# A hybrid block on one core: one more up pair in seven-product steps, three gated products on VectorE, one table load later

## The chip, the cores and the metric

The kernel runs on one NeuronCore of a Trainium2 chip. The metric is device time in microseconds (us); lower is better. Five engines work side by side, each through its own queue in order: TensorE (PE in the profile, its weight loads PEld), VectorE (DVE), ScalarE (ACT), GpSimd (POOL) and SyncE (SP, which here only issues DMAs). Operands lie in SBUF, products of TensorE land in PSUM banks.

## The reference

One layer on 512 tokens of width 1024: a short gated convolution and a forgetting attention are merged through gates, and a channel mixer follows. The change touches the mixer (FFN_HIDDEN is 2816, so 22 blocks of 128 in each half):

```python
    x = x + (g_conv * y_conv + g_attn * y_attn) @ w_o[l]
    h = rms_norm(x, norm_ffn_g[l])
    up = causal_dwconv(h @ w_up[l], conv_ffn_w[l])
    a, b = jnp.split(up, 2, axis=-1)
    x = x + (jax.nn.silu(a) * b) @ w_down[l]
    return rms_norm(x, norm_f_g)
```

## The kernel before

Tokens lie along the free axis (512), features along the partitions in blocks of 128. **Each product is made of three.** A float32 operand is split in a high part (ScalarE copies it to a rounded type, line 275: `wh_...`) and a low part (VectorE subtracts, line 279: `wl_...`); TensorE adds high x high, low x high and high x low. Weights come in chunks (`stream`, in order): a DMA of SP fills a `raw` buffer, `split` makes `wh` and `wl`, and TensorE uses them. There are two `wh` and two `wl` buffers, so the `wh` of a chunk can only be written when TensorE has finished with the `wh` of the chunk two before it.

**Plain pairs.** Pair j of the mixer is block j of `a` and block j of `b`. A plain pair is two chunks of 1024 columns, `up{2j}` and `up{2j+1}` (`block`), each 48 matmuls of 128x128 by 256 columns into one bank. VectorE then scales the bank (line 1170, `fz`), ScalarE and VectorE make the three taps of the convolution (lines 566, 567, 570, `fu`), and `glu` gates: Silu on ScalarE (line 1231), the product of an even pair on GpSimd (line 1236, `ge`), that of an odd pair too (line 1243, `go`), but for the last pair of a phase, whose product is put off and made by VectorE.

**Seven-product pairs** (those in `SUP`). Two output blocks by two input blocks by two halves of the tokens are made with seven products where a plain form takes eight. A step has a chunk P (768 columns, 18 matmuls) and a chunk F (1024 columns, 24 matmuls); a pair takes two steps, 84 matmuls in all, into the four banks 2 to 5. Their weights are sums of weight blocks. F chunks are made in DRAM by chains of DMAs, some of which add (`make_forms`: SP issues the copies at line 208, GpSimd the adds at line 211; `slot` sets when, two slots for each pair, one for each `wo` chunk in front of them and one for each down step). Their inputs are the "x forms", combinations of the rows of x1 that lie in slots 0 to 15 of `gh` and `gl` in phase 1 (`up_forms`). After the second step `merge` puts the banks together (ScalarE line 1191; VectorE lines 1192 to 1213), and the taps and `glu` follow as for a plain pair.

**Phases.** Phase 0 is pairs 0 to 11, then 12 down steps. Phase 1 is pairs 12 to 21, then the nine down steps of `STEPS[1]`, all in the seven-product form. A down step (i, q) takes as moving operands the forms of group q, that is of pairs 2q and 2q+1: seven combinations of `ge{q}` and `go{q}`, which VectorE makes (lines 1253, 1254, 1257, 1258, called t1, t3, t2, t4 below) and which are split in turn in `gh` (line 1262) and `gl` (line 1263). The first down step of phase 1 uses q = 6 and 7, the second uses q = 8 and 9, so pairs 16 to 19. Down steps are numbered through the whole program: before, those of phase 1 are P34/F34 to P42/F42.

**What sets the order.** Matmuls and conversions stand as written. Evacuations, taps and forms wait in a list `later`: each has a chunk number from which it is due and a cost in us, and `split` empties some of it behind each chunk, up to a budget (1.7 us for an `up` chunk, 1.6 for P, 0.75 for F; with evacuations waiting 4.2, 1.6 and 1.2). What a step needs is emptied at the latest by `flush` in front of it. A table load of ScalarE's Sqrt for the last norm is forced by the activation at line 1233, behind the Silu of pair 21.

Of the kernel before, what the change touches and what calls it, by code (L numbers as in the profile page):

```python
# [8 lines left out]
F32 = mybir.dt.float32  # L9
F32R = mybir.dt.float32r  # L10
AF = mybir.ActivationFunctionType
# [7 lines left out]
H = 8  # L19
# [3 lines left out]
NP = FFN // P  # L23
# [34 lines left out]
PLAIN = [(m, k) for m in (6, 7) for k in range(*PHASES[1])]  # L58
PCUTS = (0, 8, 12, 20)

SUP = ((1, 2, 5), (14, 16))
XF = (26, 0)
UPD = tuple(tuple(((j, q), (j, q + 1)) for j in js for q in (0, 2)) for js in SUP)
DOUBLES = GATES + UPD[0] + STEPS[0] + UPD[1] + STEPS[1]
# [6 lines left out]
def block_kernel(ctx, tc, xT, vecs, wv, win, wmix, wo, wup, wst, wdp, outT):  # L71
# [3 lines left out]
    nc = tc.nc  # L75
# [6 lines left out]
    def keep(ins):  # L82
        return tc.keep_in_program_order(ins)

    def bank(i, name):
        return ps.tile([P, S], F32, tag=f"b{i}", name=name)

    def ring(*ids):
        st = [0]

        def f(name):
            st[0] += 1
            return bank(ids[(st[0] - 1) % len(ids)], name)

        return f
# [13 lines left out]
    tbl = cp.tile([4 * H, 1], F32, tag="tbl", name="tbl")  # L109
# [19 lines left out]
    def step_chunks(n):  # L129
        m = len(DOUBLES[n])  # L130
        return [(f"P{n}", wst[n, :, : 3 * m * P], 3 * m * P), (f"F{n}", n, 4 * m * P)]
# [10 lines left out]
    for ph, (j0, j1) in enumerate(PHASES):  # L142
        for j in range(j0, j1):
            if j in SUP[ph]:
                stream += step_chunks(n) + step_chunks(n + 1)
# [10 lines left out]
    later = []  # L156
# [33 lines left out]
    def make_forms(n0, n1, key, start=0):  # L190

        size, step, shift = GROUPS[key]
        if not start:
            make_forms.slot = 0
        cuts = [n0]
        for n in range(n0 + 1, n1 + 1):
            if n == n1 or n - cuts[-1] == size or len(DOUBLES[n]) != len(DOUBLES[cuts[-1]]):
                cuts.append(n)
        for g, (a, b) in enumerate(zip(cuts, cuts[1:])):
            m = len(DOUBLES[a]) * P  # L200
            f = dr.tile([P, b - a, 4 * m], F32, tag=f"f{a}", name=f"f{a}")
            w = wst[a:b].rearrange("n p c -> p n c")
            x0, x1, x2 = w[:, :, 3 * m : 5 * m], w[:, :, 5 * m : 7 * m], w[:, :, 7 * m : 8 * m]
            for n in range(a, b):
                made[n] = f[:, n - a, :]

            def put(dst, src):
                return lambda: keep(nc.sync.dma_start(dst, src))

            def add(dst, src):  # L210
                return lambda: keep(nc.gpsimd.dma_start(dst, src, accum_op=ALU.add))  # L211

            f0, f1, f2 = f[:, :, : 2 * m], f[:, :, 2 * m : 3 * m], f[:, :, 3 * m :]
            ops = (put(f0, x0), add(f0, x1), put(f1, f[:, :, :m]), add(f1, x1[:, :, m:]), put(f2, f1), add(f2, x2))
            todo_bg.extend((start + (step * k if isinstance(step, int) else step[k]) + shift * g, op) for k, op in enumerate(ops))
        todo_bg.sort(key=lambda w: w[0])

    def slot():

        while todo_bg and todo_bg[0][0] <= make_forms.slot:  # L220
            todo_bg.pop(0)[1]()
        make_forms.slot += 1
# [14 lines left out]
    def flush(banks=None):  # L237

        def wanted(w):
            return set(w[2]) & set(banks) if banks is not None else True  # L240

        while any(map(wanted, later)):
            n = next(n for n, w in enumerate(later) if banks is None or wanted(w) or w[0] < len(parts))
            with after_split():
                later.pop(n)[3]()

    def flush_only(tags):

        while n := [n for n, w in enumerate(later) if set(w[2]) & set(tags)]:
            with after_split():  # L250
                later.pop(n[0])[3]()
# [84 lines left out]
    eps = ex[:, NT : NT + 1]  # L336
# [347 lines left out]
    for t in range(NT):  # L684
        src = pa[t][:, 4 * HD : VW].unsqueeze(1).to_broadcast([P, 4, H])
# [61 lines left out]
    acc, bank_s, bank_t = ring(2, 0, 1), ring(3, 4), ring(5, 6)  # L747
# [25 lines left out]
    k = len(parts) + 2  # L773
# [90 lines left out]
    acc = ring(3, 4, 5, 6, 2, 7)  # L864
# [41 lines left out]
    k = [c[0] for c in stream].index("mix0")  # L906
# [52 lines left out]
    for j in range(KB):  # L959
# [13 lines left out]
        else:  # L973
            if j == GJ:
                acc = ring(3, 4, 2, 7)
# [10 lines left out]
        a, b = gs  # L986
# [13 lines left out]
    gh = gx.tile([P, NG, 2 * P], F32R, tag="gh", name="gh")  # L1000
# [6 lines left out]
    acc = ring(0, 1, 5, 6, 3, 4, 2, 7)  # L1007
# [116 lines left out]
    def turns(*ids):  # L1124
        st = list(ids)

        def f(name):
            f.last = st.pop(0)
            flush((f.last,))
            return bank(f.last, name)  # L1130

        return f

    acc = turns(0, 1, *(2, 3, 4, 5) * 2, 6, 7, 0, 1, 2, 3, 4, 5)
    USETS = dict.fromkeys(SUP[1], (2, 3, 4, 5)) | {1: (2, 3, 4, 5), 2: (6, 7, 0, 1), 5: (6, 7, 0, 1)}
    ssq3 = xp.tile([P, S], F32, tag="ssq", name="ssq3")

    def place(ph, q):
        return (16, 24, 32, 0, 8)[q - PHASES[1][0] // 2] if ph else q * NF

    def up(j, ph, rb2, pu=None):
# [6 lines left out]

        if j in SUP[ph]:
            c = 2 * SUP[ph].index(j)  # L1150
            slot()
# [74 lines left out]
    def glu(ph, j, uu):  # L1226
        a, b = uu
        q, k = j // 2, len(parts) - 1
        g0 = place(ph, q)
        with tc.issue_after(order["hi"]) if j + 1 == PHASES[ph][1] else ExitStack():  # L1230
            nc.scalar.activation(a, a, AF.Silu)
        if j == NP - 1:
            nc.scalar.activation(tbl, a[: 4 * H, :1], AF.Sqrt, scale=0.0, bias=eps[: 4 * H])
        if j % 2 == 0:
            ge = glu.even = fp.tile([P, 2, 2 * P], F32, tag="ge", name=f"ge{q}", bufs=2)
            keep(nc.gpsimd.tensor_mul(ge, a.rearrange(halves_of, h=2), b.rearrange(halves_of, h=2)))  # L1236
            return
        flush_only([("q", x) for x in range(q)])
        ge = glu.even
        go = fp.tile([P, 6, 2 * P], F32, tag="gr", name=f"go{q}")  # L1240

        def mul(eng):
            return eng.tensor_mul(go[:, 0:2, :], a.rearrange(halves_of, h=2), b.rearrange(halves_of, h=2))

        if j + 1 < PHASES[ph][1]:
            keep(mul(nc.gpsimd))
        else:
            later.append((k + 3, 0.7, (("q", q),), lambda: mul(nc.vector)))
        b11, b12 = ge[:, 0, :], ge[:, 1, :]
        b21, b22, t1, t2, t3, t4 = (go[:, i, :] for i in range(6))  # L1250

        def t13():
            nc.vector.tensor_sub(t1, b11, b12)
            nc.vector.tensor_sub(t3, b22, b12)

        def t24():
            nc.vector.scalar_tensor_tensor(t2, t1, -1.0, b22, op0=ALU.mult, op1=ALU.subtract)
            nc.vector.scalar_tensor_tensor(t4, t2, -1.0, b21, op0=ALU.mult, op1=ALU.subtract)

        def hl(src, gs):  # L1260
            def f():
                nc.scalar.activation(gh[:, gs, :], src, AF.Copy)
                nc.vector.tensor_sub(gl[:, gs, :], src, gh.bitcast(F32)[:, gs, :])

            return f


        d = (2, 3, 4) if j + 1 < PHASES[ph][1] else (4, 5, 6)
        w = [(d[0], 0.85, t13), (d[0], 0.85, t24), (d[1], 0.7, hl(ge[:, : 1 + ph, :], slice(g0, g0 + 1 + NF * ph, NF)))]
        w += [(d[x > 0 and 2 or 1], 0.7, hl(go[:, x : x + 2, :], slice(g0 + 1 + x, g0 + 3 + x))) for x in (0, 4, 2)]  # L1270
        at = next((x for x, i in enumerate(later) if ("e",) in i[2]), len(later))
        later[at:at] = [(k + n, us, (("q", q),), f) for n, us, f in w]

    def combine(ph, i, banks, ids):

# [46 lines left out]
    X, Y = (6, 7, 0, 1), (2, 3, 4, 5)  # L1322
    for ph, (j0, j1) in enumerate(PHASES):
        if ph:
            acc = turns(*(6, 7, 0, 1) * 4)
            make_forms(ND[1], len(DOUBLES), ph)
        for j in range(j0, j1):
            pu = None
            if j == 0:
                nrm = {}  # L1330

                def mid():
                    nrm["c"] = rstd_col([ssq2], NT, 6, "n2")

                def late():
                    nrm["b"] = rstd_sb(rstd_bc(nrm["c"], NT, 7, "n2"), "n2")

                pu = lead(["up0", "up1"], x1h, x1l, mid, late)
            up(j, ph, nrm["b"], pu)
        if not ph:  # L1340
            up_forms(0, 1)
        flush_only((("e",),))
        seven(
            STEPS[ph], ND[ph], ({0: X, 1: Y, 3: X, 2: Y}, {0: X, 1: Y, 2: Y})[ph],
            lambda q, g: (gh[:, place(ph, q) + g, :], gl[:, place(ph, q) + g, :]),
            done=lambda i, banks, ids: combine(ph, i, banks, ids), tick=True,
        )
        assert not todo_bg
# [188 lines left out]
```

## Time and profile before

| | |
|---|---|
| three runs | 692.52, 692.88, 693.15 us; median 692.88 |
| the profiled execution | 693.81 us, its span 692.0 us |
| granted clock, mean | 0.998 |
| VectorE, ScalarE, GpSimd busy | 80%, 53%, 28% of the span |
| plain pairs of phase 1 | 12, 13, 15, 17, 18, 19, 20, 21 |
| seven-product pairs of phase 1 | 14, 16 |

How to read the views: in a timeline a row has its start, its length (both us), engine, line, operation, tile written <- tiles read, shapes and, in brackets, how long the engine was idle before it and who released it. Lengths of neighbouring VectorE rows overlap by about 0.08 us, so the cost of one in a full queue is the distance to the start of the next. A row of the stages has the stretch, its length, then busy us and instructions of each engine, the granted TensorE clock, the DMA share and GB/s. A row of the waits has engine, tile and line that waited, who released it, total us, times, longest. A row of the chain has start, length, engine, tile and line.

### The profile page before, as it was taken

The numbers are of one execution on the slowest core, as the hardware profiler recorded it, in microseconds if no ns is written. First come the engines' busy times: TensorE is split into PE (matmuls) and PEld (weight loads), VectorE is DVE, ScalarE is ACT, GpSimd is POOL, SyncE is SP. The second block draws the span as 40 slices with busy tenths as digits, with TensorE's granted clock in tenths as the row PEclk, the third lists the DMA queues.
The fourth block names the chain that finished last, engine by engine and source line by source line (L and its number), as shares of the span: only waits on it lengthen the run. The fifth ranks groups of instructions, "written<-read, shape, count | busy, mean of one in ns | idle before, by whom it ended". The sixth has DMA issues, their size and how long they took to land.

```text
span 692.0 us, 14716 instructions
## 1 busy us (share of the span) xinstructions
PE 683.5 (99%) x5936; PEld 681.6 (98%) x5936; DVE 554.6 (80%) x860; ACT 368.4 (53%) x581; POOL 192.8 (28%) x204
## 2 busy tenths in 40 slices
PE   9999999999999999999999999999999999999996
PEld 9999999999999999999999999999999999999996
DVE  6677887967578778868879699998786899988894
ACT  5575755555555444446554455546444544546572
POOL 6124946542020201214400144340100324332000
PEclk9999999999999999999999999999999999999999
DMA  8628999563577586798997498888944997775613
GB/s 310 219 68 286 220 241 206 127 136 92 168 160 214 162 265 196 234 310 215 165 312 237 123 252 211 190 229 254 262 141 150 314 243 169 197 168 147 205 31 123
DMA packets 66165, 137.54 MB, mean 199 GB/s; under 512 B 5888, under 2 KB 31760, under 8 KB 65840
## 3 DMA queue, kind: packets, MB, share of 16 engines
q1 hardware_dynamic: 45384, 107.28, 46.7%
q0 software_dynamic: 18896, 26.03, 23.8%
q10 hardware_dynamic: 1816, 3.29, 1.3%
q8 instruction: 46, 0.75, 0.4%
q14 instruction: 23, 0.19, 0.1%
HBM read 132.31 MB, written 47.71 MB: 260 GB/s over the span
## 4 chain that ended last, share of the span: by engine, by line
PE 88%; DVE 7%; DMA 2%; ACT 1%; issue 1%; POOL 0%; DVEq 0%; ACTq 0%; POOLq 0%
PE dn L327 26%; PE p_up L309 15%; PE p_in L309 14%; PE p_wo L309 6%; PE p_up L327 4%; PE yc L309 3%; PE ya L309 3%; PE pa L477 2%; DMA y<-ys 2%; PE pb L479 2%; PE p_q L309 2%; PE p_k L309 2%; PE o L658 2%; DVE wl_up L279 1%; PE tp L641 1%; DVE fu L567 1%
## 5 line engine op out<-in xcount | busy, mean ns | idle before, releaser
L211 POOL DMA_DIRECT2D f<-in_wst_dram x69 | 80.3, 1349 | 25.6 <-DMA f<-f 25.3
L309 PE MATMUL p_up<-x1h,wh_up 128*128 128x256 f32 x416 | 81.1, 276 | 0.0
L309 PE MATMUL p_up<-x1l,wh_up 128*128 128x256 f32 x416 | 81.1, 276 | 0.0
L309 PE MATMUL p_up<-x1h,wl_up 128*128 128x256 f32 x416 | 81.0, 276 | 0.0
L279 DVE TENSOR_TENSOR wl_F<-raw_F,wh_F 128x1024 fp32r<-128x1024 f32 (+1 forms) x43 | 56.0, 1303 | 21.6 <-ACT wh_F L275 21.6
L275 ACT ACTIVATE wh_F<-raw_F 128x1024 fp32r<-128x1024 f32 (+1 forms) x43 | 44.4, 1034 | 41.5 <-PE dn L327 27.2
L309 PEld LDWEIGHTS p_up<-x1l,wh_up 128*128 128x128 f32 x416 | 62.7, 188 | 0.0
L309 PEld LDWEIGHTS p_up<-x1h,wh_up 128*128 128x128 f32 x416 | 62.7, 188 | 0.0
L309 PEld LDWEIGHTS p_up<-x1h,wl_up 128*128 128x128 f32 x416 | 62.6, 188 | 0.0
L309 PE MATMUL p_in<-xgh,wh_in 128*128 128x256 f32 x288 | 56.8, 279 | 0.0
L309 PE MATMUL p_in<-xgh,wl_in 128*128 128x256 f32 x288 | 56.6, 278 | 0.0
L309 PE MATMUL p_in<-xgl,wh_in 128*128 128x256 f32 x288 | 56.5, 278 | 0.0
L279 DVE TENSOR_TENSOR wl_P<-raw_P,wh_P 128x768 fp32r<-128x768 f32 (+1 forms) x43 | 41.9, 974 | 13.7 <-ACT wh_P L275 7.9
L275 ACT ACTIVATE wh_P<-raw_P 128x768 fp32r<-128x768 f32 (+1 forms) x43 | 35.3, 821 | 31.2 <-PE dn L327 23.3
L1236 POOL TENSOR_TENSOR ge<-fu,fu 128x512 f32<-128x512 f32 x11 | 20.1, 1829 | 111.8 <-DVE fu L570 86.7
L327 PE MATMUL dn<-gh,wh_F 128*128 128x256 f32 x216 | 51.0, 276 | 0.0
L327 PE MATMUL dn<-gl,wh_F 128*128 128x256 f32 x216 | 51.0, 276 | 0.0
L279 DVE TENSOR_TENSOR wl_up<-raw_up,wh_up 128x1024 fp32r<-128x1024 f32 x34 | 43.8, 1288 | 7.5 <-ACT wh_up L275 7.5
L275 ACT ACTIVATE wh_up<-raw_up 128x1024 fp32r<-128x1024 f32 x34 | 35.8, 1054 | 18.3 <-PE p_up L309 8.1
L309 PEld LDWEIGHTS p_in<-xgh,wh_in 128*128 128x128 f32 x288 | 44.7, 188 | 0.7
L309 PEld LDWEIGHTS p_in<-xgl,wh_in 128*128 128x128 f32 x288 | 43.7, 188 | 0.0
L309 PEld LDWEIGHTS p_in<-xgh,wl_in 128*128 128x128 f32 x288 | 43.6, 188 | 0.0
(343 smaller groups left out, 2216.0 us busy)
## 6 DMA issues: line engine op xcount, KB each, us to landing
raw_F<-f SPq DMA_DIRECT2D x40, 512.0 KB, 5.7
raw_up<-in_wup_dram SPq DMA_DIRECT2D x34, 512.0 KB, 4.5
raw_P<-in_wst_dram SPq DMA_DIRECT2D x40, 384.0 KB, 5.6
raw_in<-in_win_dram SPq DMA_DIRECT2D x24, 512.0 KB, 3.9
f<-in_wst_dram POOLq DMA_DIRECT2D x41, 256.0 KB, 7.3
f<-in_wst_dram SPq DMA_DIRECT2D x19, 512.0 KB, 7.7
f<-in_wst_dram POOLq DMA_DIRECT2D x19, 512.0 KB, 9.1
f<-f SPq DMA_DIRECT2D x38, 256.0 KB, 6.3
```

Of the source, the lines that this page charges most:

```text
L211: return lambda: keep(nc.gpsimd.dma_start(dst, src, accum_op=ALU.add))
L275: ins = nc.scalar.activation(hi, raw, AF.Copy)
L279: ins = nc.vector.tensor_sub(lo, raw, hi.bitcast(F32))
L309: keep(nc.tensor.matmul(out[:, cs], w, x[:, cs], start=start and i == 0 and c == 0, stop=stop and i == 2 and c == len(cut) - 1,))
L327: keep(nc.tensor.matmul(out, wl if x == 1 else wh, xl if x == 2 else xh, start=opens and bk not in seen, stop=closes and bk not in left,))
L477: keep(nc.tensor.matmul(pa[t][:, :VW], xt, w[:, VB:], start=start, stop=stop))
L479: keep(nc.tensor.matmul(pb[t], xt, w[:, :VB], start=start and t % 2 == 0, stop=stop and t % 2 == 1))
L567: nc.vector.scalar_tensor_tensor(u[:, 1:], z[:, : S - 1], col(w + 1), u[:, 1:], op0=ALU.mult, op1=ALU.add)
L641: keep(nc.tensor.transpose(tp[:, ks], pt[:, ks], ident))
L658: keep(nc.tensor.matmul(o[:, 2 * P * e + c0 : 2 * P * (e + 1)], w, x[:, kb, c0:], start=e == 0 and kb == 0 and i == 0, stop=e == 1 and kb ...
L1236: keep(nc.gpsimd.tensor_mul(ge, a.rearrange(halves_of, h=2), b.rearrange(halves_of, h=2)))
```

## The change

Three edits in the mixer, and one that follows from the first.

1. Pair 18 becomes a seven-product pair (`SUP`). Its two `up` chunks of 1024 columns go, and two P and two F chunks come; the F chunks need one more group of the DMA chains. The ring of banks for the plain pairs of phase 1 has 14 entries in place of 16 (two banks for each plain pair), so pairs 19, 20 and 21 now take banks 6 and 7, 0 and 1, 6 and 7.
2. The product of an odd pair in phase 1 that stands in front of a seven-product pair (pairs 13, 15 and 17) is made by VectorE and not by GpSimd.
3. The activation that loads the root's table goes from behind the Silu of pair 21 into `later`, behind the last forms.

```diff
-SUP = ((1, 2, 5), (14, 16))
+SUP = ((1, 2, 5), (14, 16, 18))
...
-        if j == NP - 1:
-            nc.scalar.activation(tbl, a[: 4 * H, :1], AF.Sqrt, scale=0.0, bias=eps[: 4 * H])
...
-            keep(mul(nc.gpsimd))
+            keep(mul(nc.vector if ph and j + 1 in SUP[ph] else nc.gpsimd))
...
+        if j == NP - 1:
+            src = gh.bitcast(F32)[: 4 * H, g0 + 1, :1]
+            later.append((k + 10, 0, (), lambda: nc.scalar.activation(tbl, src, AF.Sqrt, scale=0.0, bias=eps[: 4 * H])))
...
-            acc = turns(*(6, 7, 0, 1) * 4)
+            acc = turns(*(6, 7, 0, 1) * 3, 6, 7)
```

Lines 1236 to 1263 of the kernel before have numbers lower by two in the changed one (the product 1241, t1 and t3 1251 and 1252, t2 and t4 1255 and 1256, the splits 1260 and 1261), and the down steps of phase 1 are called P36/F36 to P44/F44, two more than before. Three places in the queues, first before, then changed.

VectorE at the end of pair 14 (P31 and F31 are its second step; go6 belongs to pairs 12 and 13). Before:

```order
L279 TENSOR_TENSOR wl_P31_7243<-raw_P31_7046,wh_P31_7242 128x768
L1254 TENSOR_TENSOR go6_7176<-go6_7176,ge6_7043 128x256
L1257 SCALAR_TENSOR_TENSOR go6_7176<-go6_7176 128x256
L1263 TENSOR_TENSOR gl_3989<-ge6_7043,gh_3988 128x2x256
L1258 SCALAR_TENSOR_TENSOR go6_7176<-go6_7176 128x256
L279 TENSOR_TENSOR wl_F31_7273<-raw_F31_7048,wh_F31_7272 128x1024
```

Changed:

```order
L279 TENSOR_TENSOR wl_P31_7250<-raw_P31_7053,wh_P31_7249 128x768
L1241 TENSOR_TENSOR go6_7183<-fu130_7114,fu131_7178 128x512
L1261 TENSOR_TENSOR gl_3989<-ge6_7050,gh_3988 128x2x256
L1252 TENSOR_TENSOR go6_7183<-go6_7183,ge6_7050 128x256
L1255 SCALAR_TENSOR_TENSOR go6_7183<-go6_7183 128x256
L279 TENSOR_TENSOR wl_F31_7280<-raw_F31_7055,wh_F31_7279 128x1024
```

The product go6 of pair 13 now stands in VectorE's queue (fu130 and fu131 are its two inputs), and t4 stands behind the conversion of F31 and not in front of it.

VectorE at the end of phase 1, up to the conversion of the second down step's P chunk. Before, from the middle of the last splits of go9 (pairs 18 and 19; fz210, fz211 and fu210, fu211 are pair 21):

```order
L1263 TENSOR_TENSOR gl_3989<-go9_8002,gh_3988 128x512
L570 SCALAR_TENSOR_TENSOR fu201_8132<-fz201_8130,vec_64,fu201_8132 128x510
L1263 TENSOR_TENSOR gl_3989<-go9_8002,gh_3988 128x512
L1170 TENSOR_TENSOR fz210_8201<-p_up42_8152,rb_n2_4668 128x512
L279 TENSOR_TENSOR wl_P34_8274<-raw_P34_8069,wh_P34_8273 128x768
L567 SCALAR_TENSOR_TENSOR fu210_8203<-fz210_8201,vec_64,fu210_8203 128x511
L570 SCALAR_TENSOR_TENSOR fu210_8203<-fz210_8201,vec_64,fu210_8203 128x510
L1170 TENSOR_TENSOR fz211_8283<-p_up43_8220,rb_n2_4668 128x512
L279 TENSOR_TENSOR wl_F34_8280<-raw_F34_8071,wh_F34_8279 128x1024
L567 SCALAR_TENSOR_TENSOR fu211_8285<-fz211_8283,vec_64,fu211_8285 128x511
L279 TENSOR_TENSOR wl_P35_8342<-raw_P35_8140,wh_P35_8341 128x768
```

Changed, with the conversion of the first step's F chunk (wl_F36) and t1 of go9 as the two rows in front of these:

```order
L1252 TENSOR_TENSOR go9_8202<-go9_8202,ge9_8067 128x256
L1170 TENSOR_TENSOR fz210_8284<-p_up42_8139,rb_n2_4669 128x512
L1170 TENSOR_TENSOR fz211_8290<-p_up43_8212,rb_n2_4669 128x512
L1255 SCALAR_TENSOR_TENSOR go9_8202<-go9_8202 128x256
L567 SCALAR_TENSOR_TENSOR fu210_8286<-fz210_8284,vec_64,fu210_8286 128x511
L1256 SCALAR_TENSOR_TENSOR go9_8202<-go9_8202 128x256
L570 SCALAR_TENSOR_TENSOR fu210_8286<-fz210_8284,vec_64,fu210_8286 128x510
L567 SCALAR_TENSOR_TENSOR fu211_8292<-fz211_8290,vec_64,fu211_8292 128x511
L1261 TENSOR_TENSOR gl_3989<-ge9_8067,gh_3988 128x2x256
L570 SCALAR_TENSOR_TENSOR fu211_8292<-fz211_8290,vec_64,fu211_8292 128x510
L1261 TENSOR_TENSOR gl_3989<-go9_8202,gh_3988 128x512 x3
L279 TENSOR_TENSOR wl_P37_8358<-raw_P37_8121,wh_P37_8357 128x768
```

Before, all forms of go9 stand ahead of the conversion of P34, in pairs 20 and 21; now they stand between the conversions wl_F36 and wl_P37, together with the evacuation and the taps of pair 21.

TensorE in the P chunk of the second down step, from its sixth matmul to its first with the low weights. Before:

```order
L327 MATMUL dn3423_8294<-gl_3989,wh_P35_8341 128x256
L327 MATMUL dn3424_8295<-gh_3988,wh_P35_8341 128x256
L327 MATMUL dn3424_8295<-gl_3989,wh_P35_8341 128x256
L327 MATMUL dn3422_8293<-gh_3988,wh_P35_8341 128x256
L327 MATMUL dn3422_8293<-gl_3989,wh_P35_8341 128x256
L327 MATMUL dn3423_8294<-gh_3988,wh_P35_8341 128x256
L327 MATMUL dn3423_8294<-gl_3989,wh_P35_8341 128x256
L327 MATMUL dn3424_8295<-gh_3988,wl_P35_8342 128x256 [waits DVE_49]
```

Changed:

```order
L327 MATMUL dn3623_8310<-gl_3989,wh_P37_8357 128x256
L327 MATMUL dn3624_8311<-gh_3988,wh_P37_8357 128x256
L327 MATMUL dn3624_8311<-gl_3989,wh_P37_8357 128x256 [waits DVE_49]
L327 MATMUL dn3622_8309<-gh_3988,wh_P37_8357 128x256
L327 MATMUL dn3622_8309<-gl_3989,wh_P37_8357 128x256 [waits DVE_49]
L327 MATMUL dn3623_8310<-gh_3988,wh_P37_8357 128x256 [waits Activation_49]
L327 MATMUL dn3623_8310<-gl_3989,wh_P37_8357 128x256 [waits DVE_49]
L327 MATMUL dn3624_8311<-gh_3988,wl_P37_8358 128x256 [waits DVE_49]
```

The matmuls are the same; now three of them wait for VectorE and one for ScalarE ahead of the wait for the low weights.

On the other queues: SP issues two P and two F loads for pair 18 in place of two `up` loads and three more copies of the DMA chains; GpSimd issues three more adds and makes three products fewer. ScalarE has four conversions for pair 18 in place of two and one more copy (line 1191).

## Prediction

> **What bounds the kernel now.** I read the page first (busy shares, chain), then TensorE's waits, then the chain in order of time, the stages, and last the timelines of the two places where TensorE waits.
>
> ```profile
> PE 683.5 (99%) x5936; PEld 681.6 (98%) x5936; DVE 554.6 (80%) x860; ACT 368.4 (53%) x581; POOL 192.8 (28%) x204
> ...
> PE 88%; DVE 7%; DMA 2%; ACT 1%; issue 1%; POOL 0%; DVEq 0%; ACTq 0%; POOLq 0%
> ```
>
> ```profile
> PE dn L327 <- DVE wl_F L279: 0.7, 1, 0.7
> PE p_up L327 <- DVE wl_up L279: 0.2, 1, 0.2
> ```
>
> TensorE is busy 99% of the span, and 88% of the chain that ended last is its own. In the mixer it waits twice, both times for a `wl` of VectorE. So the time is the count of matmuls times their pace, plus such waits. The pace stands in the chain, at a plain block of pair 6:
>
> ```profile
> 401.22 1.36 PE p_up L327 x12
> 402.58 4.08 PE p_up L309 x36
> ```
>
> 48 matmuls take 1.36 + 4.08 = 5.44 us: 113.3 ns each. VectorE is the engine with no room. Stages of one pair each, 17, 18 and 19:
>
> ```profile
> 576.90:587.80 10.90, 10.90 (x99) 10.90 (x98) 10.67 (x19) 3.62 (x7) 7.68 (x5) 1.00 0.74 156
> 587.80:598.70 10.90, 10.90 (x98) 10.90 (x98) 10.87 (x14) 6.66 (x10) 4.56 (x5) 1.00 0.73 202
> 598.70:609.60 10.90, 10.90 (x98) 10.90 (x97) 9.76 (x17) 6.07 (x9) 4.97 (x3) 1.00 0.56 146
> ```
>
> A row has the stretch, its length and the busy time (and count) of TensorE, its weight loads, VectorE, ScalarE and GpSimd. VectorE is busy 10.67 of 10.90 us, 10.87, 9.76; idle are 0.23, 0.03 and 1.14 us. The two waits:
>
> ```profile
> 554.25 0.28 PE L327 MATMUL dn<-gl,wh_F 128*128 128x256 f32 x1
> 555.27 0.38 PE L327 MATMUL dn<-x1h,wl_F 128*128 128x256 f32 x1 [0.75 <-DVE wl_F L279]
> 555.50 0.52 PE L327 MATMUL dn<-gh,wl_F 128*128 128x256 f32 x3
> ```
>
> ```profile
> 610.29 0.28 PE L327 MATMUL p_up<-x1l,wh_up 128*128 128x256 f32 x1
> 610.72 0.73 PE L327 MATMUL p_up<-x1h,wl_up 128*128 128x256 f32 x4 [0.15 <-DVE wl_up L279]
> ```
>
> At pair 14 the matmul due at 554.36 starts at 555.27, 0.91 late, and the next one 0.23 behind it, 0.11 more than the pace. At pair 20 the one due at 610.40 starts at 610.72, 0.32 late, and again 0.11 for the restart.
>
> **The change, part by part.** Sums are made in the profiled execution's own time (span 692.0 us, run 693.81) and then put on the median of the runs, 692.88, which is 0.93 below that run.
>
> *Fewer matmuls.* The 96 of pair 18 become 84: 12 x 113.3 ns = **-1.36 us**, as long as TensorE is not kept waiting.
>
> *The product of pair 13.* Before, VectorE waits 1.19 us for GpSimd's go6, and the late `wl_F` stands behind that:
>
> ```profile
> 550.25 0.95 DVE L279 TENSOR_TENSOR wl_P<-raw_P,wh_P 128x768 fp32r<-128x768 f32 x1
> 552.39 0.42 DVE L1254 TENSOR_TENSOR go<-go,ge 128x256 f32<-128x256 f32 x1 [1.19 <-POOL go L1243]
> ...
> 554.00 1.22 DVE L279 TENSOR_TENSOR wl_F<-raw_F,wh_F 128x1024 fp32r<-128x1024 f32 x1
> ...
> 625.12 0.74 DVE L567 SCALAR_TENSOR_TENSOR fu<-fz,vec,fu 128x511 f32<-128x511 f32 x1
> 625.78 0.69 DVE L1263 TENSOR_TENSOR gl<-go,gh 128x512 fp32r<-128x512 f32 x1
> 626.39 0.74 DVE L570 SCALAR_TENSOR_TENSOR fu<-fz,vec,fu 128x510 f32<-128x510 f32 x1
> 627.05 0.68 DVE L1263 TENSOR_TENSOR gl<-go,gh 128x512 fp32r<-128x512 f32 x1
> 627.65 0.68 DVE L1170 TENSOR_TENSOR fz<-p_up,rb_n 128x512 f32<-128x512 f32 x1
> 628.25 1.45 DVE L279 TENSOR_TENSOR wl_P<-raw_P,wh_P 128x768 fp32r<-128x768 f32 x1
> ```
>
> The last six rows stand back to back and price VectorE's rows by the distance of their starts: 0.66 for a tap, 0.60 for a split of 512, 0.60 for an evacuation. The product has the same 512 columns: 0.60, near the last two. From 550.25 the `wl_P` costs 0.87; then, in the new order, product 0.60, split 0.60 and two forms of 0.34 (priced below): `wl_F` starts at 553.00 and not at 554.00. It ends at 554.22, ahead of the 554.36 at which it is wanted, so the whole 1.02 us goes. But the next conversion follows 1.15 + 0.34 + 0.60 later and ends at 556.31, and TensorE, now early, wants it 16 matmuls behind 554.36, at 556.17; with a slow restart 0.25 comes back. **-0.75**, between -1.0 and -0.4 (that the 0.60 of the product comes out as a wait).
>
> *Products of pairs 15 and 17.* 0.60 more each on VectorE, but GpSimd's product also slows VectorE beside it:
>
> ```profile
> 596.28 2.14 POOL L1243 TENSOR_TENSOR go<-fu,fu 128x512 f32<-128x512 f32 x1 [6.34 <-ACT fu L566]
> ```
>
> ```profile
> 597.19 1.78 DVE L567 SCALAR_TENSOR_TENSOR fu<-fz,vec,fu 128x511 f32<-128x511 f32 x1
> ```
>
> A tap that takes 0.74 elsewhere takes 1.78 under it. So the product of pair 17 gives back 1.0, and that of pair 15 is uncovered in VectorE's queue.
>
> *More work for VectorE in pair 18.* Conversions: two of 1.15 become two of 0.87 and two of 1.15, +1.74. Evacuation: two rows of 0.60 become `merge`, by shape four of 512 columns and three of 256, 4 x 0.60 + 3 x 0.34 = 3.4, so +2.2. With 0.60 for the product of 15 and the 1.0 given back, about 3.6 us more.
>
> This need not reach TensorE. The new queue puts pair 17's evacuation and taps and pair 18's `merge` behind the conversions of pair 18, and their banks are wanted again only by pair 20 and by the down steps. The second conversion of pair 19 can run as soon as TensorE has used the high weights of pair 18's last chunk, 104 matmuls or 11.8 us before pair 20 begins; between it and the conversion for pair 20 stand four taps (2.64), `merge` without its last row (2.8) and a product (0.60), 6.0 us. So the conversion that is late at 610.72 before is some 3 us early: **-0.43**. The delay is handed on in `later`, and where it ends up is the largest term.
>
> *The forms of pairs 18 and 19.* The second down step is the first to need them. Before, their last split is at 627.05 (above), 9 us ahead. In the new queue they follow the first step's `wl_F`, which hangs on TensorE's end of pair 21 through the `wh` buffer:
>
> ```profile
> 631.78 0.28 PE L327 MATMUL dn<-gh,wh_P 128*128 128x256 f32 x1
> ```
>
> ```profile
> 632.03 1.07 ACT L275 ACTIVATE wh_F<-raw_F 128x1024 fp32r<-128x1024 f32 x1 [2.93 <-PE p_up L309]
> ```
>
> ```profile
> 633.12 1.23 DVE L279 TENSOR_TENSOR wl_F<-raw_F,wh_F 128x1024 fp32r<-128x1024 f32 x1 [0.46 <-ACT wh_F L275]
> 634.27 0.74 DVE L567 SCALAR_TENSOR_TENSOR fu<-fz,vec,fu 128x511 f32<-128x511 f32 x1
> ...
> 642.83 0.42 DVE L1253 TENSOR_TENSOR go<-ge 128x256 f32<-128x256 f32 x1
> 643.17 0.42 DVE L1254 TENSOR_TENSOR go<-go,ge 128x256 f32<-128x256 f32 x1
> ```
>
> Count from the first matmul of the first down step (631.78 before). ScalarE's `wh_F` starts 0.25 later, `wl_F` 1.34 later, and VectorE goes on 2.49 later. Then stand, in the new order, four forms of 0.34 (the last two rows give it), two evacuations of 0.60, four taps of 0.66 and four splits of 0.60: 1.36 + 1.20 + 2.64 + 2.40 = 7.60. The second step's `wl_P` starts at 10.1 and is there 0.96 later, at 11.05. TensorE wants it after 42 + 12 matmuls, at 6.12. It comes **4.9 us late, with a restart +5.0**. Nothing hides that: TensorE's queue is in order, and three of the twelve matmuls ahead already wait for a `gl`. Behind it VectorE has conversions that wait for TensorE anyway, so it is paid once. I count ScalarE's copies and splits between as hidden, since two or more rows of VectorE stand ahead of each that is waited for; if one holds VectorE up, 5.5, and if the rows overlap a little more than the priced ones, 4.7.
>
> *The table load.* It moves in front of the `wh_P` at 652.38:
>
> ```profile
> 634.98 1.28 ACT L1233 ACT_TABLE_LOAD   x1
> ...
> 652.38 0.53 ACT L275 ACTIVATE wh_P<-raw_P 128x384 fp32r<-128x384 f32 x1 [0.48 <-PE dn L327]
> ```
>
> ScalarE is idle 0.48 there, so that conversion goes from 652.38 to about 653.4; it is wanted by the chunk P42, 210 matmuls or 23.8 us behind 631.78, at 655.6. At the old place the load lies in front of a conversion that was in time as well. Nothing in either place; uncovered 1.3.
>
> *DMAs.* Two `up` loads become two P and two F loads, SP issues three more copies and GpSimd three more adds. GpSimd is busy 28% of the span, and no wait of TensorE in the list names a DMA. Nothing; a form that came late would hold pair 18 by its F load.
>
> *The clock.* While the second step waits, TensorE gets five matmuls through in 5.6 us. Its granted clock before:
>
> ```profile
> 685.00:687.00 2.00, 0.53 (x5) 0.34 (x4) 1.43 (x3) 0.00 (x0) 0.00 (x0) 1.00 0.06 22
> 687.00:692.00 5.00, 0.00 (x0) 0.00 (x0) 1.11 (x3) 0.00 (x0) 0.00 (x0) 0.77 0.58 203
> ```
>
> TensorE stops at about 685.5; a mean of 0.77 over the last 5 us is half speed for 2.3 us, so the clock falls some 4.2 us after it stopped. [...] By the row, a gap of 4.2 us is needed and the longest single one in the walk is 2.2, so the sum leaves it out.
>
> **Sum.** -1.36 - 0.75 - 0.43 + 5.0 = +2.5: a span near 694.5, on the median **695.4 us**. With the bounds, the main case's own range is 694.8 to 696.2.
>
> **Rivals.**
> - *Faster.* The forms are not late, because VectorE does them in the room that it has behind pair 20. For it: their inputs are there by then. Against it: they stand behind a conversion that only the end of pair 21 releases. Without the +5.0 it is 690.3.
> - *Clock.* The clock falls in the stall. If half speed lasts as long as it takes to fall, 4.2 us, 2.1 us are lost on top: 697.5. For: four gaps stand close together. Against: each is under 2.3 us.
> - *VectorE bound in pairs 17 to 20.* The 3.6 us more exceed the 1.4 us idle, and from there each reaches TensorE: 2.2. The wait at pair 20 stays, and so does the stall, which starts from TensorE's own end: 692.88 - 1.36 - 0.75 + 2.2 + 5.0 = 698.0. Against: by the walk no conversion of pairs 18 to 20 is late.
> - *About even.* Half of the stall is hidden, because VectorE's rows between the conversions start earlier than the walk has them: 692.9.
>
> **Numbers.** Main case 0.66, clock 0.11, VectorE bound 0.08, even 0.07, faster 0.08. A measurement of this kernel tells about 0.2%, 1.39 us, from no change. Faster by that: 0.08. Within it (691.5 to 694.3): the even case and an edge of the main one, 0.09. Slower: 0.83. The range takes in the main case and reaches to the clock case and toward the even one: 693.9 to 697.6.
>
> **What would show it.** Right: hardly a wait at the end of pair 14, none in pairs 17 to 20, and in the chunk P37 TensorE waiting for `gl` and then for `wl_P`, 4.7 to 5.5 us in all, while VectorE is busy throughout. Wrong: P37 without a wait, waits in the `up` chunks of pairs 19 and 20, or a granted clock under 1.00 near 640 us.

## The result and the profile after

| | before | changed |
|---|---|---|
| six runs each, median | 692.82 us (692.52 to 693.35) | 697.88 us (696.71 to 698.19) |
| ratio | | 1.0065, 95% interval 1.0055 to 1.0076 |
| profiled execution, its span | 693.81, 692.0 us | 697.87, 696.1 us |
| granted clock, mean | 0.998 | 0.993 |
| TensorE's first matmul of the first down step | 631.78 us | 628.52 us |

The change makes the kernel 5.06 us slower. The forecast was 695.4, with a range to 697.6: the sign is right, the median lies 0.3 above the range. By the interval of the ratio the changed kernel stands between 696.6 and 698.1, so these runs can't tell it from the end of the range. The busy shares of the page hardly move:

```profile
PE 685.1 (98%) x5924; PEld 682.9 (98%) x5924; DVE 559.5 (80%) x870; ACT 370.2 (53%) x584; POOL 187.9 (27%) x204
```

TensorE has 12 matmuls fewer and is busy 1.6 us longer. A share cannot say why. The list of waits of the changed kernel says where:

```profile
PE dn L327 <- DVE gl L1261: 2.7, 2, 2.0
PE dn L327 <- DVE wl_P L279: 1.1, 1, 1.1
```

Both waits of before, for a `wl_F` (0.7) and a `wl_up` (0.2), are gone. All that is left in the mixer is in one chunk, P37. TensorE's timeline there:

```profile
633.97 0.28 PE L327 MATMUL dn<-gh,wh_P 128*128 128x256 f32 x1
636.23 0.38 PE L327 MATMUL dn<-gl,wh_P 128*128 128x256 f32 x1 [1.99 <-DVE gl L1261]
636.45 0.28 PE L327 MATMUL dn<-gh,wh_P 128*128 128x256 f32 x1
637.49 0.39 PE L327 MATMUL dn<-gl,wh_P 128*128 128x256 f32 x1 [0.76 <-DVE gl L1261]
637.71 0.28 PE L327 MATMUL dn<-gh,wh_P 128*128 128x256 f32 x1
638.09 0.38 PE L327 MATMUL dn<-gl,wh_P 128*128 128x256 f32 x1
639.56 1.01 PE L327 MATMUL dn<-gh,wl_P 128*128 128x256 f32 x3 [1.08 <-DVE wl_P L279]
```

Read it by the distances of the starts, not by the brackets. At the pace of 0.113 the last row would stand 6 x 0.113 = 0.68 behind the first; it stands 5.59 behind: 4.9 us are lost. The brackets add up to 3.83, because the short wait for VectorE's next `gl` (at 638.09, 0.26 behind the pace) and the slow restarts (0.22 from 636.23 to 636.45) have none. VectorE in the same stretch:

```profile
629.82 1.23 DVE L279 TENSOR_TENSOR wl_F<-raw_F,wh_F 128x1024 fp32r<-128x1024 f32 x1 [2.59 <-ACT wh_F L275]
630.97 0.42 DVE L1251 TENSOR_TENSOR go<-ge 128x256 f32<-128x256 f32 x1
631.30 0.42 DVE L1252 TENSOR_TENSOR go<-go,ge 128x256 f32<-128x256 f32 x1
631.64 1.28 DVE L1170 TENSOR_TENSOR fz<-p_up,rb_n 128x512 f32<-128x512 f32 x2
...
636.75 1.89 DVE L1261 TENSOR_TENSOR gl<-go,gh 128x512 fp32r<-128x512 f32 x3
638.55 0.95 DVE L279 TENSOR_TENSOR wl_P<-raw_P,wh_P 128x768 fp32r<-128x768 f32 x1
```

VectorE stands idle for 2.59 us in front of `wl_F`, then works without a gap until `wl_P`, 10.03 us behind the first matmul of the step (628.52). The forecast had 10.1. Then something that it did not have in its sum. Stages of the changed kernel, cut where the granted clock (the third column from the end) changes:

```profile
632.00:634.00 2.00, 2.00 (x20) 2.00 (x19) 2.00 (x5) 1.65 (x3) 0.00 (x0) 1.00 0.76 171
634.00:635.30 1.30, 0.24 (x3) 0.04 (x1) 1.30 (x3) 1.30 (x4) 0.00 (x0) 1.00 0.05 17
635.30:638.70 3.40, 1.38 (x5) 0.78 (x5) 3.40 (x7) 0.90 (x2) 0.00 (x0) 1.00 0.00 0
638.70:642.10 3.40, 2.54 (x12) 2.54 (x13) 2.74 (x3) 0.84 (x1) 0.00 (x0) 0.50 0.34 116
642.10:645.50 3.40, 3.40 (x18) 3.40 (x18) 0.77 (x2) 0.79 (x1) 0.00 (x0) 0.50 0.70 212
645.50:647.00 1.50, 1.50 (x14) 1.50 (x14) 0.87 (x1) 0.27 (x1) 0.00 (x0) 0.99 0.00 0
```

From 638.70 to 645.5 the granted clock is 0.50. In the fifth row it is "busy" all the time, yet gets 18 matmuls through in 3.40 us, 0.19 each; in the last row 14 in 1.50, 0.107 each (records that a cut divides count on both sides). The pace itself is in TensorE's timeline of the same kernel, four matmuls apart:

```profile
641.01 0.41 PE L327 MATMUL dn<-gh,wh_F 128*128 128x256 f32 x1
...
641.86 0.41 PE L327 MATMUL dn<-gh,wh_F 128*128 128x256 f32 x1
```

(641.86 - 641.01) / 4 = 0.213 us in place of 0.113. Before, the granted clock was 1.00 in the whole of the down steps (631.8 to 667.6 us). Of the 6.8 us at half clock the matmuls from 639.56 on fill 6.0, a loss of 6.0 x (1 - 0.113/0.213) = 2.8 us.

### The profile page after: what moved, and what is told of

Its sections match the earlier page's. It is cut to its first block, busy times and chain, and to the rows that moved or that the text cites. A ratio compares the mean times of both kernels' runs of the same rounds, so it can differ in the third digit from the quotient of the medians.

```text
span 696.1 us, 14723 instructions
## 1 busy us (share of the span) xinstructions
PE 685.1 (98%) x5924; PEld 682.9 (98%) x5924; DVE 559.5 (80%) x870; ACT 370.2 (53%) x584; POOL 187.9 (27%) x204
## 5 line engine op out<-in xcount | busy, mean ns | idle before, releaser
L309 PE MATMUL p_up<-x1h,wh_up 128*128 128x256 f32 x392 | 76.5, 276 | 0.0
L309 PE MATMUL p_up<-x1h,wl_up 128*128 128x256 f32 x392 | 76.3, 276 | 0.0
L309 PE MATMUL p_up<-x1l,wh_up 128*128 128x256 f32 x392 | 76.3, 276 | 0.0
L309 PEld LDWEIGHTS p_up<-x1h,wh_up 128*128 128x128 f32 x392 | 59.1, 188 | 0.0
L309 PEld LDWEIGHTS p_up<-x1h,wl_up 128*128 128x128 f32 x392 | 59.0, 188 | 0.0
L309 PEld LDWEIGHTS p_up<-x1l,wh_up 128*128 128x128 f32 x392 | 59.0, 188 | 0.0
L327 PE MATMUL dn<-gl,wh_F 128*128 128x256 f32 x228 | 55.4, 281 | 0.0
L327 PE MATMUL dn<-gh,wh_F 128*128 128x256 f32 x228 | 55.3, 281 | 0.0
L327 PEld LDWEIGHTS dn<-gh,wh_F 128*128 128x128 f32 x228 | 43.9, 193 | 0.0
L327 PEld LDWEIGHTS dn<-gl,wh_F 128*128 128x128 f32 x228 | 43.9, 193 | 0.0
```

What stands on the lines that cost most here:

```text
L309: keep(nc.tensor.matmul(out[:, cs], w, x[:, cs], start=start and i == 0 and c == 0, stop=stop and i == 2 and c == len(cut) - 1,))
L327: keep(nc.tensor.matmul(out, wl if x == 1 else wh, xl if x == 2 else xh, start=opens and bk not in seen, stop=closes and bk not in left,))
```

## The experiments

All stand against the changed kernel, if nothing else is said. Its median, 697.88, and that of before, 692.82, are from the runs above; in the experiments' own comparisons the kernel before had medians of 693.08, 692.90 and 692.87. The changed kernel was not run again beside them, so differences from it of a few tenths say little.

### 1. Without pair 18

```diff
-SUP = ((1, 2, 5), (14, 16, 18))
+SUP = ((1, 2, 5), (14, 16))
...
-            acc = turns(*(6, 7, 0, 1) * 3, 6, 7)
+            acc = turns(*(6, 7, 0, 1) * 4)
```

> The change without its first part: pair 18 stays in plain blocks; the products of pairs 13 and 15 on VectorE and the table load at its new place stay. My theory: the whole loss sits in the second down step and comes from pair 18's delay on VectorE, so nothing of it is here, and only the wait of TensorE for wl_F at the end of pair 14 goes: 692.8 - 0.75 = 692.1, between 691.8 and 692.4; no wait in the second down step, granted clock 1.00 up to the root. Rival one, the products on VectorE or the table load are what delays the forms: slower than before, 694 or more. Rival two, the product is worth nothing since another wait takes its place: 692.8.

Measured 692.68 us (692.40 to 693.63); ratio to before 0.9995, 0.9986 to 1.0003: no difference that can be told. The wait at the end of pair 14 is gone, as expected, but TensorE's timeline at pair 20 now reads:

```profile
609.94 0.72 PE L327 MATMUL p_up<-x1h,wl_up 128*128 128x256 f32 x4 [0.76 <-DVE wl_up L279]
```

Before, the wait at this place was 0.15 in its bracket; by the starts the matmul was 0.32 late, and is now 0.92. So of the 1.02 won at pair 14, 0.6 is given back at pair 20, because the conversion that TensorE waits for starts only 0.78 earlier (608.67, before 609.45). What holds it back was not tested; VectorE, with almost no idle time in pairs 17 to 19 and the product of pair 15 added to its queue, is the likely cause. My expectation missed this. The stall and the fall of the clock are not here (the granted clock is 1.00 from 620 to 650 us): the loss needs pair 18.

### 2. The forms of pairs 18 and 19 early

```diff
             if i and j + 1 == PHASES[ph][1]:
                 split_next()
+                flush_only((("q", 9),))
                 split()
```

> The change, with the forms of pairs 18 and 19 put in front of the low weights of the first down step's second chunk (wl_F) in VectorE's queue. No work is added or left out. My theory: these forms stood behind a conversion that only TensorE's end of pair 21 releases; ahead of it they fill the 2.6 us that VectorE stood idle there. By the rows wl_F then starts some 30.8 - 28.5 = 2.3 us behind the first matmul of the step, is there at 3.5 (wanted at 3.85), and the next wl_P is there at 5.5 (wanted at 6.1): the stall of 4.9 and the half clock of about 2.8 behind it both go, 697.9 - 7.7 = 690.2, between 689.6 and 691.0. Rival, VectorE simply has too much work from pair 18 on: the wait moves to wl_F of the first step or stays at wl_P, 694 to 698.

Measured 690.52 us (690.41 to 691.11); ratio to before 0.9967, 0.9955 to 0.9979. One line turns a loss of 5.06 into a gain of 2.3, with the same work on every engine. VectorE in this version:

```profile
628.36 1.89 DVE L1262 TENSOR_TENSOR gl<-go,gh 128x512 fp32r<-128x512 f32 x3
630.17 1.22 DVE L279 TENSOR_TENSOR wl_F<-raw_F,wh_F 128x1024 fp32r<-128x1024 f32 x1
631.30 1.28 DVE L1171 TENSOR_TENSOR fz<-p_up,rb_n 128x512 f32<-128x512 f32 x2
632.50 0.95 DVE L279 TENSOR_TENSOR wl_P<-raw_P,wh_P 128x768 fp32r<-128x768 f32 x1
633.37 1.40 DVE L567 SCALAR_TENSOR_TENSOR fu<-fz,vec,fu 128x511 f32<-128x511 f32 x2
634.69 1.40 DVE L570 SCALAR_TENSOR_TENSOR fu<-fz,vec,fu 128x510 f32<-128x510 f32 x2
```

The forms stand in the time in which VectorE stood idle in the changed kernel, and `wl_P` starts 4.57 behind the first matmul of the step (627.93 here), not 10.03. The forms are not all that left its queue: the four taps of pair 21, which stood among them, now come behind `wl_P` (the last two rows). At the prediction's prices the forms are 3.76 of the difference and the taps 2.64, and `wl_F` starts 0.94 later: 3.76 + 2.64 - 0.94 = 5.46. The granted clock is 1.00 from 620 to 650 us. What TensorE still loses there:

```profile
630.11 0.38 PE L327 MATMUL dn<-gh,wh_F 128*128 128x256 f32 x1
...
637.28 0.51 PE L327 MATMUL dn<-gh,wl_F 128*128 128x256 f32 x2 [0.31 <-DVE wl_F L279]
```

The first is 0.25 late with its restart, the second 0.59. The rival, VectorE simply overloaded, falls: it had the time, but in the wrong place.

### 3. The second and the third down step exchanged

```diff
-    (((2, 6), (2, 7)), ((2, 8), (2, 9)), ((0, 6), (0, 7)),
+    (((2, 6), (2, 7)), ((0, 6), (0, 7)), ((2, 8), (2, 9)),
```

> The change, with the second and the third down step exchanged, so that the forms of pairs 18 and 19 are first needed one step (4.8 us) later; VectorE's queue stays as it is, instruction by instruction. My theory: what sets the end of the stall is the length of VectorE's queue up to wl_P of the second step (10.0 us behind the first matmul of the first step, there at 11.0), not the forms as such; the 12 high products now go through without a wait, then one wait of 4.9 us in one piece, and the clock falls as before or by more: 697 to 699. Rival, the late forms (gl) are the cause, as the list of waits puts it (2.7 us on gl, 1.1 on wl_P): without them 1.1 us stays and the clock does not fall: 692.5 to 693.5.

Measured 697.33 us (696.20 to 697.47); ratio to before 1.0058, 1.0044 to 1.0072. TensorE in the second down step, which no longer needs the late forms:

```profile
634.24 0.28 PE L327 MATMUL dn<-gl,wh_P 128*128 128x256 f32 x1
639.26 1.65 PE L327 MATMUL dn<-gh,wl_P 128*128 128x256 f32 x6 [4.75 <-DVE wl_P L279]
```

The 12 high products go through, then one gap of 5.02, 4.9 more than the pace. The list of waits of the changed kernel gave `gl` 2.7 and `wl_P` 1.1; here `gl` has nothing and `wl_P` 4.8. So the list names who came last in each piece of a wait. What set the end was the queue of VectorE in front of `wl_P`, which this edit does not touch. Stages:

```profile
634.70:638.10 3.40, 0.00 (x0) 0.00 (x0) 3.40 (x6) 1.21 (x3) 0.00 (x0) 1.00 0.00 0
638.10:641.50 3.40, 2.24 (x10) 2.24 (x11) 2.74 (x4) 0.84 (x1) 0.00 (x0) 0.50 0.32 105
641.50:645.00 3.50, 3.50 (x19) 3.50 (x18) 1.07 (x2) 0.59 (x1) 0.00 (x0) 0.51 0.68 217
```

The clock falls as in the changed kernel, to 0.50, and for as long (3.4 and 3.5 us, there 6.8 in all).

### 4. Forty matmuls more in the stall

```diff
+            if name == "P37":
+                dum = bank(0, "dum")
+                for x in range(40):
+                    keep(nc.tensor.matmul(dum[:, th[0]], x1h[:, 0, :P], x1h[:, 0, th[0]], start=True, stop=True))
             passes(out, len(out))
```

> The change, with 40 matmuls more in front of the second down step's first product, into a bank that is free there and that nothing reads: 40 x 113 ns = 4.5 us of added work where TensorE waited 4.9. My theory: the gaps of that stall cost twice, once as a wait and once as half clock for 6.8 us behind it. With TensorE kept busy the step's first low product starts as before, 11.0 us behind the first step, but the granted clock stays 1.00 and 2.7 to 3.0 us come back: 694.9 to 695.3, faster with more work. Rival, the clock fell for another reason, or its fall costs nothing since other engines set the pace there: 697.9 or more.

Measured 695.01 us (694.64 to 696.28); ratio to before 1.0031, 1.0020 to 1.0042. More work, and 2.9 us less time. TensorE's timeline and a stage of it:

```profile
632.77 4.96 PE L859 MATMUL dum<-x1h 128*128 128x256 f32 x40
...
639.04 0.98 PE L327 MATMUL dn<-gh,wl_P 128*128 128x256 f32 x6
```

```profile
638.00:641.00 3.00, 3.00 (x26) 2.89 (x25) 3.00 (x5) 0.85 (x1) 0.00 (x0) 1.00 0.30 93
```

The second step starts 4.76 behind the first, so the first low product comes 639.04 - 632.77 + 4.76 = 11.03 us behind the first step's start, as in the changed kernel (639.56 - 628.52 = 11.04). Nothing of the wait was removed, only filled; what goes is the half clock (1.00 in the stage above). The loss of 5.06 thus has two parts of their own: the late `wl_P`, and 2.7 (by the spans, 696.1 and 693.4) to 2.9 (by the medians) for the clock that fell meanwhile.

### 5. The products back on GpSimd

```diff
-            keep(mul(nc.vector if ph and j + 1 in SUP[ph] else nc.gpsimd))
+            keep(mul(nc.gpsimd))
```

> The change without its second part: the products of pairs 13, 15 and 17 are GpSimd's again; pair 18 in seven-product steps and the table load as in the change. My theory: VectorE waits for GpSimd's product of pair 13 again and TensorE is 1.0 late at the end of pair 14, as before the change; the delay reaches the end, since the stall in the second down step counts from TensorE's own arrival: 697.9 + 1.0 = 698.9, between 698.4 and 699.5. Rival, drawn from the run without pair 18 (where the 1.0 won at pair 14 came back as 0.6 more at pair 20): the product is worth 0.4 or nothing: 697.9 to 698.3.

Measured 697.74 us (696.97 to 698.89); ratio to before 1.0068, 1.0056 to 1.0081. The forecast of 698.4 to 699.5 was missed. In the trace TensorE waits again at the end of pair 14, 0.51 and 0.11 for the restart, but the times of this kernel and of the changed one lie over each other, each spread over some 1.5 us or more. As a test of the second part it is inconclusive; experiment 9 repeats it where the times scatter less.

### 6. The table load at its old place

```diff
             nc.scalar.activation(a, a, AF.Silu)
+        if j == NP - 1:
+            nc.scalar.activation(tbl, a[: 4 * H, :1], AF.Sqrt, scale=0.0, bias=eps[: 4 * H])
...
-        if j == NP - 1:
-            src = gh.bitcast(F32)[: 4 * H, g0 + 1, :1]
-            later.append((k + 10, 0, (), lambda: nc.scalar.activation(tbl, src, AF.Sqrt, scale=0.0, bias=eps[: 4 * H])))
```

> The change without its third part: the table load behind the Silu of pair 21 again. My theory: ScalarE issues it after its last copy of the late forms and then stands idle 3.4 us before its next conversion, so the load (1.3 us) is hidden in both places: 697.9, within 0.4. Rival, the load delays what VectorE waits for: up to 1.3 more, 699.2.

Measured 697.21 us (696.92 to 697.85); ratio to before 1.0060, 1.0045 to 1.0076. The load takes 1.28 us on ScalarE, behind its last copy of the late forms, and the next conversion there is in any case released later. The median is 0.7 below that of the changed kernel, outside the 0.4 that I had allowed, and inside the spread of its runs. The waits of TensorE are the same to 0.1. The load costs nothing that can be told, in either place.

### 7. Taps of pair 21 behind the next conversion

The version of experiment 2, with the taps of the last half of pair 21 due one chunk later (`glu` counts its own due numbers from where it did):

```diff
+            if j == NP - 1 and i:
+                due = len(parts) + 1
+                evac[0][1]()
+                later.extend((due, us, (("q", 10),), f) for us, f in evac[1:])
-            if any(("e",) in w[2] for w in later):
+            elif any(("e",) in w[2] for w in later):
...
-        q, k = j // 2, len(parts) - 1
+        q, k = j // 2, len(parts) - 1 - 2 * (j == NP - 1)
```

> The change, with the forms of pairs 18 and 19 early as in the second experiment, and the taps of the last half of pair 21 behind the low weights of the second down step's second chunk. My theory: in the second experiment TensorE still waits 0.6 for that wl_F (late behind four taps); two of them moved behind it, it is there 1.3 earlier and the wait goes: 690.5 - 0.6 = 689.9. Rival, the last product and its forms come late instead and TensorE waits at the fifth down step: 690.5 or more.

Measured 690.85 us (690.30 to 690.92); ratio to before 0.9966, 0.9954 to 0.9979: no faster than experiment 2. In VectorE's queue three taps, not two, stand behind that `wl_F`, which starts at 634.03 and not at 636.01. The wait for it (0.59) is gone; at the fifth down step there is a new one:

```profile
645.20 0.37 PE L327 MATMUL dn<-gl,wh_P 128*128 128x256 f32 x1
645.41 0.28 PE L327 MATMUL dn<-gh,wh_P 128*128 128x256 f32 x1
645.79 0.39 PE L327 MATMUL dn<-gl,wh_P 128*128 128x256 f32 x1
646.02 0.28 PE L327 MATMUL dn<-gh,wl_P 128*128 128x256 f32 x1
```

Three distances of 0.21, 0.38 and 0.23 in place of 0.113 are 0.48 lost. The rival was right: the last product and its forms are late instead.

### 8. Twenty matmuls in place of forty

As experiment 4, with `range(20)`.

> As the run with 40 matmuls more in front of the second down step, with 20: 2.3 us of added work, so that the waits that are left sum to 2.6 us, in single gaps up to about 1 us. Here two readings of the clock differ. One: the clock falls when TensorE has been idle for most of a stretch of some 3.4 us (the records change only at multiples of 3.41 us); then it stays full, 695.0 as with 40. The other: any gap of about 1 us is enough; then it falls as in the change: 697.9.

Measured 695.41 us (694.72 to 698.39); ratio to before 1.0042, 1.0026 to 1.0059. Neither forecast holds for all five runs. Three lie near the first (694.72 to 695.41), one between the two (696.09), one above the second (698.39). The mean granted clock was 0.997 in the first three and 0.995 in the other two, which fits a fall in two executions of five; only the one at 696.09 has a profile. In it the clock did fall, though for half as long (3.4 us):

```profile
632.00:635.50 3.50, 3.50 (x32) 3.50 (x31) 3.50 (x7) 3.50 (x6) 0.00 (x0) 1.00 0.31 82
635.50:638.90 3.40, 1.81 (x11) 1.21 (x10) 3.40 (x6) 0.23 (x1) 0.00 (x0) 1.00 0.00 0
638.90:642.30 3.40, 3.20 (x15) 3.21 (x16) 2.74 (x4) 0.84 (x1) 0.00 (x0) 0.50 0.57 143
642.30:645.00 2.70, 2.70 (x25) 2.70 (x25) 0.55 (x2) 1.06 (x1) 0.00 (x0) 1.00 0.67 235
```

In the stretch ahead of the fall nine matmuls start (the count of 11 has two from before the cut): 9 x 0.113 = 1.0 of its 3.4 us. So TensorE was idle for 2.4 of the 3.4 us, in waits of at most 1.1 by its list of waits: the condition of the first reading was met, and my conclusion from it, that 20 matmuls keep the clock full, was wrong. The second reading fails by the wait of before at pair 14, which was 0.91 us: the granted clock is 1.00 around it and behind it (550 to 610 us).

### 9 and 10. The products, in the version with early forms

The version of experiment 2 with the edit of experiment 5, and beside it that version as it is.

> The version of the second experiment (forms of pairs 18 and 19 early), with the products of pairs 13, 15 and 17 back on GpSimd. Without the clock's fall the times scatter less, so the worth of the second part can be told here. My theory: the wait of TensorE at the end of pair 14 that came back in the fifth experiment's trace, 0.51 + 0.11 = 0.6, comes back here and reaches the end: 0.6 slower than the same version with the products on VectorE, 691.1 beside 690.5. Rival, the delay meets a later wait that shrinks by as much (as it did in the run without pair 18): no difference, 690.5.

> The version of the second experiment once more, as it is, on the same chip as the run before it, so that the two differ by the products alone: 690.5, between 690.2 and 691.1.

Measured 691.65 us (691.23 to 692.73), ratio to before 0.9978, 0.9969 to 0.9987, and 690.76 us (690.28 to 690.84), ratio 0.9964, 0.9951 to 0.9977. The two groups of runs do not meet: the products on VectorE are worth 0.9 us. The trace with them on GpSimd, VectorE's row and TensorE's:

```profile
551.39 0.43 DVE L1253 TENSOR_TENSOR go<-go,ge 128x256 f32<-128x256 f32 x1 [1.19 <-POOL go L1242]
```

```profile
554.28 0.38 PE L327 MATMUL dn<-x1h,wl_F 128*128 128x256 f32 x1 [0.35 <-DVE wl_F L279]
```

By the starts TensorE loses 0.62 there. With the products on VectorE (experiment 10) it loses 0.16 a little later, and the two profiles differ by 0.40 more behind pair 14 than in front of it. They keep that difference to the end of the pairs, as the theory has it; the other 0.5 of the medians is not placed. That the product was worth little without pair 18 (experiment 1) and more with it is a point at which the parts of the change depend on each other: the gain at pair 14 is kept only if the conversion for pair 20 is no longer the next thing that is late.

## Why the prediction was half right

**Fewer matmuls, pair 20.** Right: 5924 matmuls in place of 5936, and no wait at pair 20 (0.43).

**The product of pair 13.** Forecast 0.75, for 1.02 less a new wait of 0.25 at the conversion behind. In the profiled execution of the change the whole 1.02 went and no wait came; in that of experiment 10 one of 0.16 did. Experiments 9 and 10 give 0.9 by their medians and 0.4 by the place in their profiles; both lie within the term's bounds of 0.4 and 1.0. Together with the two terms above the first down step starts 3.26 earlier, where the forecast had 2.54. 0.27 of the difference is this term. The other 0.45 lies in no single gap: in the profile of before TensorE's pace is slower in three stretches, from 473, 555 and 611 us on. For example, the eight matmuls from 556.32 to 557.27 take 0.119 each, and in the changed kernel, from 555.09 to 555.99, 0.113. By the starts of the same matmuls in both profiles the three stretches are worth 0.19, 0.17 and 0.09. The first lies in the down steps of phase 0, whose matmuls the change leaves as they are. Why the pace falls stays open.

**VectorE's extra work in pair 18.** Right that it does not reach TensorE in pairs 17 to 20: there is no wait there. The rival "VectorE bound" (698.0) gives nearly the measured time for a wrong reason, which the list of waits and experiment 2 rule out.

**The late forms.** Right in place, cause and size: `wl_P` starts 10.03 behind the step's first matmul (forecast 10.1), the stall is 4.9 (forecast 4.9 and 0.1 for a restart). Experiment 3 shows that the queue in front of `wl_P` is the cause, experiment 2 that the forms, with the taps that stand among them, are what made it long. With the clock at 1.00 (experiment 4) the kernel takes 695.01, 0.4 from the forecast of 695.4. The rival "faster" was priced at 690.3 for the case that the forms come in time; made so, they give 690.5.

**Table load and DMAs at nothing.** Right as far as the runs can tell (experiment 6; no wait of TensorE names a DMA).

**The clock.** Here the prediction failed, at this step: "By the row, a gap of 4.2 us is needed and the longest single one in the walk is 2.2, so the sum leaves it out." The longest gap was 2.26, as walked, and the clock fell all the same, 4.7 us behind the start of the first gap; experiment 4 prices it at 2.7 to 2.9. The row of 4.2 was one fall after one long gap, and I made a threshold for single gaps of it, though the stretch as a whole had five matmuls in it. The rival for the clock had 0.11 and 2.1 us, for half speed of 4.2 us; it lasted 6.8. So the prediction had named what happened, with its own sign (a granted clock under 1.00 near 640 us), but left it out of the sum.

With that term the account closes to 0.1 to 0.3 us. On the medians, by the forecast's own terms: -2.54 + 4.9 + 2.8 = +5.2, measured +5.06. On the profiled executions: -3.26 + 4.9 + 2.8 = +4.4, by the spans +4.1. The two differ because the profiled execution of before (693.81) lay 0.99 above the median of its six runs and that of the change (697.87) at its own.

## What to carry over

When work is added to an engine whose queue is in order, don't only ask whether it has the time; look for the next instruction in that queue that waits for somebody else, and see what lands behind it. A delay that was harmless in front of it becomes a stall behind it, and moving the delayed work ahead costs nothing if the engine was idle there. When TensorE loses some microseconds, price the clock too: read the granted clock of the stages, and the idle time summed over a stretch, not only the longest gap. Here the clock fell to 0.50 behind stretches of 3.4 us in which at most nine matmuls started, of some 30 that fit at 0.113 each, and stayed at 1.00 behind one in which 19 did.

## What the runs showed of the hardware

- In the changed kernel's profile the granted clock is 1.0 for 631.47 us, 0.5 for 6.83 and 1.0 for 47.79, until it is 0.5 in the tail. These are 185, 2 and 14 times 3.413 us, half of the 6.83. In experiment 8 it is 0.5 for one stretch of 3.4.
- Not every stretch ahead of a fall was idle throughout. Those ahead of the three falls in the down steps, of 3.4 us each, had 5 matmuls (0.6 us of work, changed kernel), none (experiment 3) and nine (1.0 us, experiment 8). The stretch in front of the first of these, 631.88 to 635.29 us in the changed kernel, had 19 (2.2 us), and the clock was 1.00 behind it. What happens between nine and 19 was not measured.
- Of the stretches of 3.4 us at 0.50, one with 12 matmuls was followed by another at 0.50 (changed kernel), one with 15 by 1.00 (experiment 8); at 0.213 each some 16 fit.
- That the fall of the clock is what spreads the changed kernel's runs over 1.5 us, and those of experiment 8 over 3.7, was not shown: of the versions whose profiled execution has a mean clock of 0.996 to 0.999 (0.993 in the changed kernel, 0.995 in experiment 8), experiments 2, 7 and 10 spread over 0.6 to 0.7, but experiments 1, 4 and 9 over 1.2 to 1.6, and the kernel before, in two of its sets, over 2.8.
